# PEER block of 512 tokens on one core: 352 tokens dense and 160 gathered instead of 384 and 128, and V rows stationary in the last matmuls

## The chip, the cores and the metric

One core of a Trainium2 chip runs the whole program; the other cores are idle. The metric is the device time of one execution in microseconds (us), median of several runs.

## The reference, cut to what matters

Two residual blocks run over 512 tokens of width 1024. The change touches only the last part of the second block, a feed-forward layer with 16384 experts (PEER): every token picks 16 experts in each of 8 heads, applies one row of U and one row of V per expert, and sums.

```python
def peer_ffn(h, w_query, sub_keys, u_tab, v_tab):
    q = (h @ w_query).reshape(bsz, seq, 8, 2, 128)
    scores = jnp.einsum('blhcd,hckd->blhck', q, sub_keys)      # 128 keys per half
    s_top, i_top = lax.top_k(scores, 16)
    cand_s = s_top[..., 0, :, None] + s_top[..., 1, None, :]   # 16 x 16 pairs
    cand_i = i_top[..., 0, :, None] * 128 + i_top[..., 1, None, :]
    best_s, pos = lax.top_k(cand_s, 16)
    expert_idx = take_along_axis(cand_i, pos); gates = softmax(best_s)
    # per token: 8 x 16 experts
    act = gelu(einsum('td,thkd->thk', h, u_tab[expert_idx]))
    return einsum('thk,thkd->td', gates * act, v_tab[expert_idx])
x = x + peer_ffn(rms_norm(x), ...)
```

## The kernel before

Everything up to the residual `x3` (features on partitions, 512 tokens along the row) is the same before and after and is not described. What follows computes the PEER layer in two ways at once.

**Dense tokens.** The first TD = 384 tokens are run against all experts. Experts come in NB = 128 blocks of 128. In the U stage each block j is one projection of 8 k-tiles and 3 matmuls each (`mm3`: high weight by high and by low activation, low weight by high activation, so that the products come out in nearly full precision), 24 matmuls with the tokens as moving columns; a gelu writes `act`, which goes to DRAM (`AD`) for 96 blocks and stays in SBUF for the last 32 (`keep`). In the V stage each block n takes its `act`, multiplies it with the gates of the block (`Gg`, zero where a token did not choose the expert), splits the product `w` into `wth` and `wtl`, and multiplies with the 128 rows of V. There `wth` and `wtl` are stationary and the V rows move, 512 columns at a time: for 3 token tiles, 3 products and 2 halves of the width 18 matmuls, into 6 banks of PSUM (`acc`), which are summed over all 128 blocks.

**Gathered tokens.** The last 128 tokens are one token per partition. For each of their 128 choices an indirect DMA on GpSimd's queue (`rows`) fetches one row of U per token, 128 rows of 4 KB; VectorE makes the dot product with `hN` (`gather`), and later scales a row of V and adds it to `accN` (`gather_v`). Ahead of each fetch GpSimd copies one column of a recent `act` into the buffer, which holds the fetch back until that block is done (`pace`); in the V stage this copy is left out. RB = 8 buffers hold fetched rows.

**Routing.** `query` and `scores` compute the 16 query tiles and, on VectorE, the top 16 keys. `choose(t)` picks the experts of token tile t on VectorE, with one product on GpSimd; `dense_gates(t)` builds the gates of a dense tile in DRAM (`GD`), 32 tokens at a time, by four VectorE products (L1428) and 8 small matmuls per 4 tokens (L1411, L1412).

**Weights.** Each 128x1024 weight tile is loaded by a DMA on SyncE's queue (`raw`), rounded by ScalarE (`whi`, L114), and the rest is taken by VectorE (`wlo`, L115). TensorE waits for both.

**Order.** A scheduler orders each engine's queue from the program order and its own cost model. In the program order, every U block also runs RATE_R steps of the routing and RATE_U steps of the gather, every V block RATE_V steps of the gather (`Fill.run`); each step of the gather is one fetch and the use of a fetch made six steps earlier. Until the gathered tokens are routed, a U block runs 3 routing steps.

```python
RATE_R, RATE_U, RATE_V = 1.15, 1.2, 1.08
Gx = Fill(itertools.chain(gather(), gather_v()))
```

Of the kernel before, what the change touches and what calls it, by code (L numbers as in the profile page):

```python
# [26 lines left out]
RB, OB, ABUFS = 8, 2, 3  # L27
# [6 lines left out]
RATE_R, RATE_U, RATE_V = 1.15, 1.2, 1.08  # L34
# [38 lines left out]
def tile_kernel(ctx: ExitStack, tc: tile.TileContext, I, out, dump=None, stop=None):  # L73
# [1159 lines left out]
    TD = 384  # L1233
    NTD = TD // 128
# [6 lines left out]
    hN = gt.tile([128, D], F32, name="hN")  # L1241
    accN = gt.tile([128, D], F32, name="accN")
# [7 lines left out]
    x3d = dr.tile([NTD, 128, D], F32, name="x3d")  # L1250
# [12 lines left out]
    def rows_of_x3(t):  # L1263
        o = accN if t == NTD else n3.tile([128, D], F32, name="x3T", tag="x3T", bufs=2)
# [5 lines left out]
        if t == NTD:  # L1270
            nc.vector.scalar_tensor_tensor(hN, accN, r3[:, t:t + 1], gB, op0=OP.mult, op1=OP.mult)
        else:
            nc.scalar.dma_start(x3d[t], o)

    for t in (NTD, *range(NTD)):
        rows_of_x3(t)
# [50 lines left out]
    def choose(t):  # L1327
# [38 lines left out]
        for i in range(2):  # L1366
            o = rt(f"ii{i}", [8, 16])
            for q in range(2):
                hs = slice(4 * q, 4 * q + 4)
                eq = rt("eq", [4, 16, 16], bufs=2)  # L1370
# [13 lines left out]
        if t == NTD:  # L1384
            nc.vector.tensor_tensor(out=gat.rearrange("p (h k) -> p h k", h=8), in0=g,
                                    in1=gs[:, :, None].to_broadcast([128, 8, 16]), op=OP.mult)
            nc.vector.scalar_tensor_tensor(g.rearrange("p h k -> p (h k)"), res[1], 128.0, res[0],
                                           op0=OP.mult, op1=OP.add)
            nc.vector.tensor_copy(idx, g.rearrange("p h k -> p (h k)"))
            return  # L1390
# [3 lines left out]
        ts = slice(t * 128, (t + 1) * 128)  # L1394
# [4 lines left out]
        nc.scalar.activation(f(R1), pt[:, 0:128], AF.Copy)  # L1399
        nc.scalar.activation(f(R2), pt[:, 128:256], AF.Copy)  # L1400
        nc.scalar.activation(f(GH), pt[:, 256:384], AF.Copy)
        nc.vector.tensor_tensor(out=f(GL), in0=pt[:, 256:384], in1=f(GH), op=OP.subtract)
        yield

    late = []

# [11 lines left out]
    def dense_gates(t, rg):  # L1418
        nb = 128 // GT
        for tb in range(nb * t, nb * t + nb):  # L1420
# [14 lines left out]
        while len(late) > (0 if t == NTD - 1 else 2):  # L1435
            g_mm(*late.pop(0))

    def route():
# [4 lines left out]
        yield from choose(0)  # L1443
        for t in range(NTD):
            nxt = choose(t + 1) if t + 1 < NTD else iter(())
# [7 lines left out]
    def rows(tab, at, paced=True):  # L1453
# [8 lines left out]
    dense_v = []  # L1462

    def gather():
        ready = []
        for k in range(128 + RB - 2):
            if k < 128:
                ready.append((k, rows("peer_u_rows", idx[:, k:k + 1])))
            if k >= RB - 2:
                n, r = ready.pop(0)  # L1470
                nc.vector.scalar_tensor_tensor(r, r, 1.0, hN, op0=OP.mult, op1=OP.mult, accum_out=dot[:, n:n + 1])  # L1471
                if n % 16 == 15:
                    s = slice(n - 15, n + 1)
                    nc.scalar.activation(dot[:, s], dot[:, s], GELU)
                    nc.vector.tensor_tensor(out=dot[:, s], in0=dot[:, s], in1=gat[:, s], op=OP.mult)
            yield

    def gather_v():

        ready = []  # L1480
        for k in range(128 + RB - 2):
            if k < 128:
                ready.append((k, rows("peer_v_rows", idx[:, k:k + 1], not dense_v)))
            if k >= RB - 2:
                n, r = ready.pop(0)
                nc.vector.scalar_tensor_tensor(accN, r, dot[:, n:n + 1], accN, op0=OP.mult, op1=OP.add)  # L1486
            yield

# [43 lines left out]
    for jg in range(NB // AJ):  # L1532
# [11 lines left out]
        for jj in range(AJ):  # L1544
# [10 lines left out]
            if on:  # L1555
                Gx.run(RATE_U)
# [4 lines left out]
    dense_v.append(1)  # L1561
# [140 lines left out]
```

## Time and profile before

| | us |
|---|---|
| median of 3 runs (2893.13 to 2897.28) | 2893.77 |
| the profiled execution, its own time | 2892.62 |
| its span in the trace | 2890.8 |
| outside the span | 1.8 |
| query stage, U stage, V stage, rest (from the trace) | 102.9, 645.8, 559.3, 4.1 |

The stages are those of TensorE: the first matmul of the queries stands at 1578.7 us, the first of U at 1681.6, the first of V at 2327.4, and the last ends at 2886.7. TensorE is busy 96% of the span, VectorE 73%, ScalarE 40%, GpSimd 17%.

### The profile page before, as it was taken

The page shows a single profiled execution, that of the slowest core. Times are in us where ns is not written, and L with a number is a line of the kernel's source. Part 1 is how long each engine was busy: PE and PEld are TensorE (multiplying, and loading weights), DVE is VectorE, ACT ScalarE, POOL GpSimd, SP SyncE. Part 2 cuts the span into 40 slices and gives each one's busy share as a digit, 9 for nine tenths or more (in the row PEclk, how much of TensorE's full clock was granted, in tenths as well). Part 3 has the DMA queues.
Part 4 walks back from the last instruction along what each step waited for, and adds up shares of the span by engine and source line. Part 5 has one row for each costly group of instructions (what it writes and reads, how often), then busy time and mean ns, then how long its engine had stood idle before and what let it go on. Part 6 is the DMA issues. An engine that isn't in the chain of part 4 may idle for free.

```text
span 2890.8 us, 37068 instructions
## 1 busy us (share of the span) xinstructions
PE 2785.8 (96%) x13917; PEld 2280.5 (79%) x13917; DVE 2099.1 (73%) x3645; ACT 1159.4 (40%) x1599; POOL 492.2 (17%) x452
## 2 busy tenths in 40 slices
PE   7999999999999999999999988999998989999999
PEld 5777888877888866656687888898998978777887
DVE  5786894339777665777544999999785579988554
ACT  4667523224333343333433334555553333333332
POOL 0000000000000000000000016546343357652000
PEclk8999999999999999999999999999999999999999
DMA  6333263333333332222233237898899699999663
GB/s 246 122 112 109 97 196 106 124 114 105 97 92 96 89 124 73 73 73 66 75 102 116 88 126 267 299 340 310 323 330 337 234 349 380 401 390 347 216 214 116
DMA packets 167476, 540.11 MB, mean 187 GB/s; under 512 B 16896, under 2 KB 42112, under 8 KB 163840
## 3 DMA queue, kind: packets, MB, share of 16 engines
q1 hardware_dynamic: 128128, 391.94, 39.7%
q0 software_dynamic: 36864, 134.23, 12.5%
q10 hardware_dynamic: 2304, 11.57, 1.1%
q8 instruction: 109, 1.79, 0.2%
q14 instruction: 71, 0.58, 0.1%
HBM read 479.48 MB, written 58.20 MB: 186 GB/s over the span
## 4 chain that ended last, share of the span: by engine, by line
PE 74%; DVE 10%; issue 6%; DMA 5%; POOL 3%; ACT 3%; SPq 0%; DVEq 0%; POOLq 0%; ACTq 0%
PE pmm L122 15%; PE pmm L124 15%; PE pmm L123 15%; PE acc L1604 13%; DMA raw<-in_peer_v_rows_dram 3%; DVE wlo L115 2%; PE pmm L1002 2%; POOL rows L1458 2%; DVE rows L1471 1%; PE pm L209 1%; PE pa L151 1%; POOL rows L1457 1%; PE pg L122 1%; PE pg L123 1%; ACT whi L114 1%
## 5 line engine op out<-in xcount | busy, mean ns | idle before, releaser
L114 ACT ACTIVATE whi<-raw 128x1024 fp32r<-128x1024 f32 (+2 forms) x502 | 518.1, 1033 | 1023.3 <-PE pmm L123 773.4
L115 DVE TENSOR_TENSOR wlo<-raw,whi 128x1024 fp32r<-128x1024 f32 (+2 forms) x502 | 608.0, 1212 | 283.5 <-ACT whi L114 278.9
L124 PE MATMUL pmm<-nph,wlo 128*128 128x384 f32 (+1 forms) x1152 | 398.9, 347 | 20.3 <-DVE wlo L115 20.2
L122 PE MATMUL pmm<-nph,whi 128*128 128x384 f32 (+1 forms) x1152 | 405.7, 352 | 0.3 <-ACT whi L114 0.3
L123 PE MATMUL pmm<-npl,whi 128*128 128x384 f32 (+1 forms) x1152 | 397.5, 345 | 0.0
L1604 PE MATMUL acc<-whi,wth 128*128 128x512 f32 x768 | 243.0, 397 | 7.3 <-ACT whi L114 7.3
L1604 PE MATMUL acc<-wlo,wth 128*128 128x512 f32 x768 | 243.6, 398 | 6.2 <-DVE wlo L115 6.1
L124 PEld LDWEIGHTS pmm<-nph,wlo 128*128 128x128 f32 x1152 | 220.3, 191 | 29.9 <-DVE wlo L115 24.8
L1604 PE MATMUL acc<-whi,wtl 128*128 128x512 f32 x768 | 242.6, 397 | 0.0
L122 PEld LDWEIGHTS pmm<-nph,whi 128*128 128x128 f32 x1152 | 220.6, 192 | 5.1 <-ACT whi L114 0.6
L123 PEld LDWEIGHTS pmm<-npl,whi 128*128 128x128 f32 x1152 | 220.4, 191 | 4.5
L1458 POOL DMA_INDIRECT rows<-in_peer_v_rows_dram,idx x128 | 202.0, 1578 | 108.5 <-DVE accN L1486 97.5
L1471 DVE SCALAR_TENSOR_TENSOR rows<-rows,hN 128x1024 f32<-128x1024 f32 x128 | 155.1, 1218 | 55.3 <-DMA rows<-in_peer_u_rows_dram,idx 55.3
L1486 DVE SCALAR_TENSOR_TENSOR accN<-rows,dot,accN 128x1024 f32<-128x1024 f32 x128 | 163.7, 1279 | 27.3 <-DMA rows<-in_peer_v_rows_dram,idx 27.0
L1604 PEld LDWEIGHTS acc<-wlo,wth 128*128 128x128 f32 x768 | 143.8, 188 | 45.8 <-DVE wlo L115 11.0
L1604 PEld LDWEIGHTS acc<-whi,wth 128*128 128x128 f32 x768 | 144.6, 189 | 44.3 <-ACT whi L114 9.2
L1604 PEld LDWEIGHTS acc<-whi,wtl 128*128 128x128 f32 x768 | 144.8, 189 | 35.8
L1458 POOL DMA_INDIRECT rows<-in_peer_u_rows_dram,idx x128 | 164.0, 1281 | 48.6 <-POOL rows L1457 26.0
L144 ACT ACTIVATE wth<-w 128x384 fp32r<-128x384 f32 x128 | 66.7, 522 | 244.0 <-PE acc L1604 223.7
L145 DVE TENSOR_TENSOR wtl<-w,wth 128x384 fp32r<-128x384 f32 x128 | 70.8, 554 | 101.9 <-ACT wth L144 101.9
L122 PE MATMUL pmm<-h2h,whi 128*128 128x512 f32 x352 | 139.2, 397 | 2.1 <-ACT h2h L186 2.0
L124 PE MATMUL pmm<-h2h,wlo 128*128 128x512 f32 x352 | 138.0, 394 | 2.8 <-DVE wlo L115 2.8
(492 smaller groups left out, 5855.8 us busy)
## 6 DMA issues: line engine op xcount, KB each, us to landing
raw<-in_peer_u_dram SPq DMA_DIRECT2D x128, 512.0 KB, 5.3
raw<-in_peer_v_rows_dram SPq DMA_DIRECT2D x128, 512.0 KB, 6.2
GD<-G SPq DMA_DIRECT2D x12, 2048.0 KB, 11.4
Gg<-GD SPq DMA_DIRECT2D x64, 384.0 KB, 8.5
raw<-in_w_up_dram SPq DMA_DIRECT2D x44, 512.0 KB, 3.5
AD<-act SPq DMA_DIRECT2D x48, 384.0 KB, 6.4
act<-AD SPq DMA_DIRECT2D x48, 384.0 KB, 7.0
raw<-in_w_mod_dram SPq DMA_DIRECT2D x32, 512.0 KB, 3.9
```

Of the source, the lines that this page charges most:

```text
L114: nc.scalar.activation(hi[:, :n], raw[:, :n], AF.Copy)
L115: (eng or nc.vector).tensor_tensor(out=lo[:, :n], in0=raw[:, :n], in1=hi[:, :n].bitcast(F32), op=OP.subtract)
L122: nc.tensor.matmul(ps, wh, ah, start=first, stop=False)
L123: nc.tensor.matmul(ps, wh, al, start=False, stop=False)
L124: nc.tensor.matmul(ps, wl, ah, start=False, stop=last)
L144: nc.scalar.activation(hi, src, AF.Copy)
L145: nc.vector.tensor_tensor(out=lo, in0=src, in1=hi.bitcast(F32), op=OP.subtract)
L1002: nc.tensor.matmul(py[32 * i:32 * i + 32], CD[c][:, s], x, start=n == 0, stop=n == 3)
L1458: nc.gpsimd.indirect_dma_start(out=r, out_offset=None, in_=I[tab], in_offset=bass.IndirectOffsetOnAxis(ap=at, axis=0))
L1471: nc.vector.scalar_tensor_tensor(r, r, 1.0, hN, op0=OP.mult, op1=OP.mult, accum_out=dot[:, n:n + 1])
L1486: nc.vector.scalar_tensor_tensor(accN, r, dot[:, n:n + 1], accN, op0=OP.mult, op1=OP.add)
L1604: nc.tensor.matmul(acc[t][q], a[:, c], bb[:, q * 512:(q + 1) * 512], start=f, stop=l)
```

## The change

352 tokens are dense and 160 gathered. The 32 new gathered tokens (the last 32 rows of tile 2) have 128 choices each; they are put on all 128 partitions as four groups of 32 choices, so that they take 32 fetches of 128 rows more in each of U and V, and their four partial sums are added at the end. The dense matmuls have 352 moving columns in place of 384 in U. In V the rows of V become stationary (8 tiles of 128 features) and `wth`, `wtl` move, 24 matmuls of 352 columns per block into 8 banks, features on partitions; at the end the result is copied out and transposed back. The gates have 11 groups of 32 tokens, not 12. The low halves of the query weights and of the first U block (17 tiles) are made on GpSimd. The fetches in V are held back too, by a mark that ScalarE makes from each `wth`. The routing order becomes tile 3, 2, 0, 1; the rates change; there are 9 row buffers; `eq` is fp16; `hN` and `accN` share a buffer.

```diff
-RB, OB, ABUFS = 8, 2, 3
+RB, OB, ABUFS = 9, 2, 3
-RATE_R, RATE_U, RATE_V = 1.15, 1.2, 1.08
+RATE_R, RATE_U, RATE_U2, RATE_V = 1.25, 1.1, 1.7, 1.45
-    TD = 384
-    NTD = TD // 128
+    TD = 352
+    NTD = 3
+    TX = 128 * NTD - TD
...
     def rows_of_x3(t):
...
+        elif t == NTD - 1:
+            p = slice(128 - TX, 128)
+            nc.vector.scalar_tensor_tensor(hX[p], o[p], r3[p, t:t + 1], gB[p], op0=OP.mult, op1=OP.mult)
+            for c in range(3):
+                nc.scalar.dma_start(hX[TX * c:TX * c + TX], hX[p])
+        nc.scalar.dma_start(x3d[t], o)
...
-            get_w(*(("w_query", x) if x < 16 else ("peer_u", x - 16)))
+            get_w(*(("w_query", x) if x < 16 else ("peer_u", x - 16)), eng=nc.gpsimd)
...
+            for c in range(4):
+                for d, x in ((idxX, ix), (gatX, ga)):
+                    nc.gpsimd.dma_start(d[TX * c:TX * c + TX], x[128 - TX:128, 32 * c:32 * c + 32])
...
-        for tb in range(nb * t, nb * t + nb):
+        for tb in range(nb * t, min(nb * t + nb, NTB)):
...
-        if paced:
-            nc.gpsimd.tensor_copy(r[:, 0:1], pace[0])
+        nc.gpsimd.tensor_copy(r[:, 0:1], pace[0])
...
+    places = [(idx, gat, dot, k) for k in range(128)] + [(idxX, gatX, dotX, k) for k in range(32)]
...
     def gather_v():
+        accN = gt.tile([128, D], F32, name="accN", tag="hN")
+        nc.gpsimd.dma_start(accN, x3d[NTD])
+        accX = gt.tile([128, D], F32, name="accX", tag="hX")
+        nc.gpsimd.memset(accX, 0.0)
+        nc.gpsimd.dma_start(accX[0:TX], x3d[NTD - 1, 128 - TX:128])
...
+        for c in range(1, 4):
+            r = gt.tile([128, D], F32, name="rows", tag="rows", bufs=RB)
+            nc.gpsimd.dma_start(r[0:TX], accX[TX * c:TX * c + TX])
+            nc.vector.tensor_tensor(out=accX[0:TX], in0=accX[0:TX], in1=r[0:TX], op=OP.add)
+        nc.gpsimd.dma_start(out[TD:128 * NTD], accX[0:TX])
...
-                Gx.run(RATE_U)
+                Gx.run(RATE_U2 if R.done else RATE_U)
...
-    acc = [[ps.tile([128, 512], F32, name=f"acc{t}{q}", bufs=1) for q in range(2)] for t in range(NTD)]
+    acc = [ps.tile([128, 512], F32, name=f"acc{k}", tag=f"acc{k}", bufs=1) for k in range(KT)]
...
+        m = vp.tile([128, 1], F32, name="mark", tag="mark", bufs=16)
+        nc.scalar.activation(m, wth[:, 0:1].bitcast(F32), AF.Copy)
+        marks.append(m)
...
-        for t in range(NTD):
-            c = slice(t * 128, (t + 1) * 128)
-            for a, bb, f, l in ((wth, vh, n == 0, False), (wth, vl, False, False), (wtl, vh, False, n == NB - 1)):
-                for q in range(2):
-                    nc.tensor.matmul(acc[t][q], a[:, c], bb[:, q * 512:(q + 1) * 512], start=f, stop=l)
+        pace[0] = marks[max(n - 2, 0)]
+        last.append((n, w, wth, wtl, vh, vl))
+        if n != NB - 2:
+            for k in range(KT):
+                s = slice(k * 128, (k + 1) * 128)
+                for m, _, wth, wtl, vh, vl in last:
+                    pq = acc[k][:, :TD]
+                    nc.tensor.matmul(pq, vh[:, s], wth, start=m == 0, stop=False)
+                    nc.tensor.matmul(pq, vh[:, s], wtl, start=False, stop=False)
+                    nc.tensor.matmul(pq, vl[:, s], wth, start=False, stop=m == NB - 1)
+                if n == NB - 1:
...
+                    if k % 2:
+                        nc.vector.tensor_copy(yT[:, k], acc[k][:, :TD])
+                    else:
+                        nc.scalar.activation(yT[:, k], acc[k][:, :TD], AF.Copy)
+            last.clear()
         Gx.run(RATE_V)
     Gx.run(1000)
-    nc.sync.dma_start(out[TD:T], accN)
...
+            for k in range(4):
+                nc.tensor.transpose(pt[:m, k * 128:(k + 1) * 128], yT[:, 4 * q + k, t * 128:t * 128 + m], ident)
...
+            nc.vector.tensor_tensor(out=x3[:m, t, c], in0=pt[:m], in1=x3[:m, t, c], op=OP.add)
+            nc.sync.dma_start(out[t * 128:t * 128 + m, c], x3[:m, t, c])
```

## Rows read from the trace of the kernel before

**Rows 1.** The page: the span, and each engine's busy time, share and instructions

```profile
span 2890.8 us, 37068 instructions
...
PE 2785.8 (96%) x13917; PEld 2280.5 (79%) x13917; DVE 2099.1 (73%) x3645; ACT 1159.4 (40%) x1599; POOL 492.2 (17%) x452
```

**Rows 2.** Windows: length, busy us of PE, PEld, DVE, ACT, POOL; clock, DMA, GB/s

```profile
1578.70:1681.60 102.90, 102.12 (x514) 86.36 (x513) 95.99 (x478) 37.20 (x56) 0.00 (x0) 1.00 0.28 93
1681.60:2002.00 320.40, 291.15 (x1864) 279.49 (x1863) 317.37 (x739) 151.57 (x192) 163.81 (x146) 0.96 0.78 277
2002.00:2192.00 190.00, 178.22 (x1221) 170.20 (x1220) 155.37 (x233) 97.92 (x125) 82.37 (x89) 0.97 0.91 330
2192.00:2327.40 135.40, 134.43 (x773) 134.11 (x772) 73.26 (x84) 47.21 (x67) 47.00 (x61) 0.99 0.76 267
2327.40:2380.00 52.60, 43.65 (x175) 33.23 (x174) 38.32 (x47) 14.75 (x21) 32.51 (x23) 0.97 1.00 378
2380.00:2644.00 264.00, 259.46 (x1092) 205.63 (x1091) 248.05 (x285) 93.72 (x123) 160.47 (x95) 0.99 1.02 390
2450.00:2550.00 100.00, 99.62 (x426) 79.40 (x425) 94.59 (x109) 34.14 (x45) 67.84 (x40) 1.00 1.03 398
2644.00:2886.70 242.70, 242.67 (x1041) 194.14 (x1039) 129.70 (x173) 84.10 (x111) 0.00 (x0) 1.00 0.59 193
```

**Rows 3.** Timeline of TensorE's matmuls in the U stage: start, duration, instruction

```profile
1990.32 0.33 PE L124 MATMUL pmm<-nph,wlo 128*128 128x384 f32 x1
...
1992.39 0.34 PE L124 MATMUL pmm<-nph,wlo 128*128 128x384 f32 x1
...
1993.02 0.42 PE L122 MATMUL pmm<-nph,whi 128*128 128x384 f32 x1
1993.28 0.34 PE L123 MATMUL pmm<-npl,whi 128*128 128x384 f32 x1
```

**Rows 4.** Timeline of TensorE's matmuls in the V stage

```profile
2700.31 0.63 PE L1604 MATMUL acc<-whi,wth 128*128 128x512 f32 x2
...
2704.98 0.39 PE L1604 MATMUL acc<-wlo,wth 128*128 128x512 f32 x1
```

**Rows 5.** Timeline of TensorE's matmuls of 256 columns, in the attention part

```profile
1114.83 0.28 PE L1064 MATMUL pmm<-wlo,hbh 128*128 128x256 f32 x1
...
1115.78 0.28 PE L1063 MATMUL pmm<-whi,hbh 128*128 128x256 f32 x1
```

**Rows 6.** Timeline of the weight loads of those matmuls

```profile
1114.83 0.19 PEld L1065 LDWEIGHTS pmm<-whi,hbl 128*128 128x128 f32 x1
```

**Rows 7.** TensorE's waits in the U stage: us in total, times, longest

```profile
PE pmm L124 <- DVE wlo L115: 20.2, 10, 6.6
```

**Rows 8.** Windows of VectorE's gate products (L1428) alone, 1681.6 to 2192

```profile
1681.60:2192.00 510.40, 132.68 (x192) 0.97 0.83 296
```

**Rows 9.** Timeline of VectorE in the V stage

```profile
2441.60 1.22 DVE L115 TENSOR_TENSOR wlo<-raw,whi 128x1024 fp32r<-128x1024 f32 x1
2442.74 0.55 DVE L1583 TENSOR_TENSOR w<-keep,Gg 128x384 f32<-128x384 f32 x1
2443.20 1.28 DVE L1486 SCALAR_TENSOR_TENSOR accN<-rows,dot,accN 128x1024 f32<-128x1024 f32 x1
2444.40 0.55 DVE L145 TENSOR_TENSOR wtl<-w,wth 128x384 fp32r<-128x384 f32 x1
```

**Rows 10.** Groups of GpSimd in the whole span: busy us, mean ns

```profile
L1373 POOL TENSOR_TENSOR eq<-eq,idf 128x1024 f32<-128x1024 f32 x12 | 36.2, 3021 | 26.1 <-DVE eq L1371 26.1
```

**Rows 11.** Groups of GpSimd in the V stage

```profile
L1458 POOL DMA_INDIRECT rows<-in_peer_v_rows_dram,idx x115 | 189.3, 1646 | 104.0 <-DVE accN L1486 97.5 <-issue 6.0 <-DVE wtl L145 0.3
```

**Rows 12.** Timeline of transposes ahead of the queries, and of the last instructions

```profile
1573.94 5.02 PE L1268 MATMUL pmm<-ident,x 128*128 128x128 f32 x32
...
2883.68 4.09 DVE L1611 TENSOR_TENSOR x3b<-acc,x3b 128x512 f32<-128x512 f32 x6 [7.25 <-PE acc L1604]
```

**Rows 13.** The page's DMA issues: KB each, us to landing

```profile
Gg<-GD SPq DMA_DIRECT2D x64, 384.0 KB, 8.5
```

More of the change, by code (lines that the diff above doesn't have):

```diff
@@ L1263, in rows_of_x3 @@
     def rows_of_x3(t):
-        o = accN if t == NTD else n3.tile([128, D], F32, name="x3T", tag="x3T", bufs=2)
+        o = n3.tile([128, D], F32, name="x3T", tag="x3T", bufs=2)
         for q in range(2):
@@ L1270, in rows_of_x3 @@
         if t == NTD:
[L1271 to L1275, printed above, removed]
+            nc.vector.scalar_tensor_tensor(hN, o, r3[:, t:t + 1], gB, op0=OP.mult, op1=OP.mult)
+        elif t == NTD - 1:
[4 more added lines that the diff above has]
+        nc.scalar.dma_start(x3d[t], o)
+    for t in range(NTD, -1, -1):
         rows_of_x3(t)
@@ L1434, in dense_gates @@
                     yield
-        while len(late) > (0 if t == NTD - 1 else 2):
+        while len(late) > (0 if t == seq[-1] else 2):
             g_mm(*late.pop(0))
@@ L1442, in route @@
         rg = rx_.enter_context(tc.tile_pool(name="rg", bufs=1, side="right", reuse_waits="tile"))
-        yield from choose(0)
-        for t in range(NTD):
-            nxt = choose(t + 1) if t + 1 < NTD else iter(())
+        yield from choose(seq[0])
+        for n, t in enumerate(seq):
+            nxt = choose(seq[n + 1]) if n + 1 < NTD else iter(())
             for i, _ in enumerate(dense_gates(t, rg)):
@@ L1460, in rows @@
         return r
[L1462 removed]
+    places = [(idx, gat, dot, k) for k in range(128)] + [(idxX, gatX, dotX, k) for k in range(32)]
     def gather():
         ready = []
[L1466 to L1468 removed]
+        for k in range(len(places) + RB - 2):
+            if k < len(places):
+                ix, ga, do, n = places[k]
+                ready.append((ga, do, n, rows("peer_u_rows", ix[:, n:n + 1])))
@@ L1476, in gather @@
             yield
     def gather_v():
+        accN = gt.tile([128, D], F32, name="accN", tag="hN")
[3 more added lines that the diff above has]
+        nc.gpsimd.dma_start(accX[0:TX], x3d[NTD - 1, 128 - TX:128])
         ready = []
-        for k in range(128 + RB - 2):
-            if k < 128:
-                ready.append((k, rows("peer_v_rows", idx[:, k:k + 1], not dense_v)))
+        for k in range(len(places) + RB - 2):
+            if k < len(places):
+                ix, ga, do, n = places[k]
+                ready.append((do, n, rows("peer_v_rows", ix[:, n:n + 1])))
@@ L1484, in gather_v @@
             if k >= RB - 2:
-                n, r = ready.pop(0)
-                nc.vector.scalar_tensor_tensor(accN, r, dot[:, n:n + 1], accN, op0=OP.mult, op1=OP.add)
-            yield
+                do, n, r = ready.pop(0)
+                a = accN if do is dot else accX
+                nc.vector.scalar_tensor_tensor(a, r, do[:, n:n + 1], a, op0=OP.mult, op1=OP.add)
+            if k == 128 + RB - 2:
+                nc.gpsimd.dma_start(out[128 * NTD:T], accN)
+            yield
+        for c in range(1, 4):
+            r = gt.tile([128, D], F32, name="rows", tag="rows", bufs=RB)
+            nc.gpsimd.dma_start(r[0:TX], accX[TX * c:TX * c + TX])
+            nc.vector.tensor_tensor(out=accX[0:TX], in0=accX[0:TX], in1=r[0:TX], op=OP.add)
```

62 lines of the change are left out of this document (36 added, 26 removed).

## The prediction

> **What bounds the kernel now.** I read the page first: TensorE's matmuls are busy 96% of the span, VectorE 73%, ScalarE 40% [rows 1], so the question is what TensorE does and why it idles. Then the windows by stage [rows 2]. The reader is to see three regimes there. In the U stage up to 2002 us VectorE is busy 317.4 of 320.4 us, so it sets the pace; from 2002 to 2192 both are high; from 2192, where the gates are done, TensorE alone is full (134.4 of 135.4). In the V stage until 2644, as long as gathered rows come in, DMA is at a share of 1.00 to 1.03 and VectorE at 94% of 2380 to 2644; after that TensorE is full and all else has room. The waits say the same: TensorE's longest wait in U is for VectorE's low halves of the weights, 20.2 us, up to 6.6 us at a time [rows 7].
>
> Then the timelines, for the period from one matmul's start to the next, since the listed durations overlap. 384 columns: 12 periods between 1990.32 and 1992.39, 0.1725 us each [rows 3]. 512 columns in V: 20 periods in 4.67 us, 0.2335 us [rows 4]. 256 columns: 8 periods in 0.95 us, 0.119 us [rows 5].
>
> **The matmuls.** From 256 to 384 columns the period grows by 0.00042 us a column, so 352 columns should take 0.159 us, 24 of them 3.82 us. A U block takes 24 x 0.1725 = 4.14 now. A V block takes 18 x 0.2335 = 4.20. By the slope 512 columns would take 0.226; in V they take 0.007 more, where every matmul goes to another bank than the last. After the change the bank changes at every third, at most 8 x 0.007 = 0.06 a block: 3.82 to 3.88, I take 3.85. So TensorE's own work falls by 128 x 0.32 = 41 us in U and 128 x 0.35 = 45 us in V. The gate matmuls of 4 tokens cost 0.545 us (0.89 from 1992.39 to 1993.28 less two periods) [rows 3]; 88 in place of 96 save 4 us.
>
> One rule speaks against this. In the last part of U the weight loads are busy 134.1 of 135.4 us, and V goes from 18 to 24 loads a block [rows 2]. The Trainium skill ("Perfetto Trace Analysis", Identifying the Most-Contended Engine) takes the busy share of weight loads as the measure of TensorE's headroom, and by it U has none. A load is listed with 0.19 us but follows the last after 0.119 us where the matmuls have 256 columns [rows 5, 6], so loads overlap one another, and I don't take them as a bound; the case is rival 3.
>
> **The U stage, by VectorE.** In program order the routing has 109 steps after the gathered tokens are routed at block 3, done at 1.15 a block by block 95 or so. With 11 token groups it has 102, and at 1.25 is done by block 84. Up to 2192 VectorE was busy 317.4 + 155.4 = 472.8 of 510.4 us, 92.6% [rows 2]. Off this go: 12 low halves (84 blocks, not 96) at 1.14 from start to start, 14 us [rows 9]; some 21 dot products (1.1 x 81 = 89 against 110) at 1.20, the price of the like operation in V, 25 us [rows 9]; a twelfth of the gate products' 132.7 us, 11 us [rows 8]; and the lag with which VectorE enters the stage. In the query stage it was 96.0 of 102.9 us busy [rows 2], 16 low halves (18 us) of which go to GpSimd; I take 8 us of lag saved, bounds 0 and 18. Left are 415 us. TensorE needs 84 x 3.82 + 88 x 0.545 = 369 in this part, so VectorE still sets it: 415 if it never idles, 448 at the 92.6% of before; I take 432. The new rates ask for more VectorE work per block than before, which is why the gain of the matmuls is not all kept here.
>
> The other 44 blocks: the 32.2 blocks (773/24) after 2192 took 4.20 each against 4.14 of matmuls, 1.5% more [rows 2]. So 44 x 3.82 x 1.015 = 171 us. At 1.7 fetches a block VectorE needs 1.14 + 1.7 x 1.20 = 3.2 of 3.82 us, and DMA 0.524 x 2.7 = 1.42 MB, 370 GB/s, under the 398 that the trace shows [rows 2]. U: 432 + 171 = 603 us in place of 645.8, bounds 583 (415 + 168) and 628 (448 + 180).
>
> **The V stage.** 5 steps of the U gather and 167 of the V gather are left, at 1.45 a block 119 of the 128 blocks. Per block in that time: TensorE 3.85; VectorE 1.14 for the low half, 2 x 0.46 x 352/384 for `w` and `wtl`, 1.45 x 1.20 for the adds, 3.74 us [rows 9]; DMA 0.524 MB of V rows, 0.760 of gathered rows, 0.180 of gates (a block's share of four 384 KB loads, less a twelfth) and 0.135 of `act`, 1.60 MB [rows 13], which at 398 GB/s is 4.02 us. That 398 was moved while TensorE was 99.6% and VectorE 94.6% busy [rows 2], with GpSimd waiting for VectorE to free row buffers (97.5 us in all) [rows 11], so it is not shown to be the ceiling. VectorE at 94.6% gives 3.95, between 3.85 and 4.02; I take that. 119 x 3.95 + 9 x 3.85 = 505, and 5 for the start, where TensorE idled 9 of 52.6 us while fetches ran unheld [rows 2]. 510 us against 559.3. Bounds: 495 with TensorE never waiting, and 119 x 4.50 + 35 = 570 at the pace of before, which made 70.4 blocks (1267/18) in the 316.6 us with gathers [rows 2].
>
> The whole stage moves 119 x 1.60 + 9 x 0.5, some 195 MB. The Trainium skill ("HBM Reference", Specifications) gives a core some 358 GB/s, by which V would take an estimated 545 us and the sum would be 2837; the 398 of rows 2 is above that, and the page itself lets a core that streams alone go higher.
>
> **What costs nothing, and under what cover.** GpSimd's 17 low halves: 3.02 us each by its nearest product [rows 10], 51 us in a stage of 102.9 in which it did nothing [rows 2]; a tile is prepared two query tiles ahead, over 10 us, and if that cover is gone each costs up to 1.9 us more than on VectorE. I take 1 us gained before U, bounds 3 either way. `hX` and its three DMAs on ScalarE's queue wait for VectorE; behind them stand the next copies, with ScalarE 36% busy [rows 2]: 0, at most 3. The eight small DMAs of choices stand on GpSimd's queue and wait for `choose`; behind them wait fetches, and behind those dot products. GpSimd is half busy there [rows 2], and the buffers hold 7 fetches, some 30 us: 0, at most 10. `accN` and `accX` are loaded on GpSimd's queue between the last U dot and the first V fetch: the 7 steps without a fetch cover it. The marks are one ScalarE column a block: 0. SyncE loses one output DMA to GpSimd.
>
> **The end.** Now 4.1 us pass after the last matmul. After: a copy of 0.55, 12 transposes at 5.02/32 = 0.16, an add of 0.68 [rows 12], 3 us of landing as now, latencies: 6.5.
>
> **Sum**, against the profiled execution's 2892.6 (1.1 under the median): 1680.6 to U, 603, 510, 6.5, and 1.8 outside the span: 2802 us.
>
> **Rivals.** 1. TensorE sets both stages: VectorE at 100% in U (583), 495 in V, in all 2767. For it: from 2450 to 2550 TensorE was 99.6% busy at a DMA share of 1.03 [rows 2]. Against: VectorE at 97%, DMA and TensorE must then all fit within 3.85 us. 2. The gather takes the gain of V: a fetch late by DMA stops VectorE in its queue, then low halves, then TensorE, and V keeps 4.50 a block: 570, in all 2862. For it: DMA at 1.03 already and 25% more rows; against: fetches are now held back, so no bursts. 3, the other side: weight loads bind. At 0.188 us each a block costs 4.51 in both stages: U 432 + 44 x 4.51 = 630, V 128 x 4.51 + 5 = 582, in all 2901, slower. It decides in V from 0.175 us a load (4.20/24); rows 5 show 0.119. 4. The gather outlasts the matmuls: the 115 fetches in V took 2.75 us each before (in 316.6 us) [rows 11], by which 165 take 454 us; 12 us of sums at the end leave 498, so it shows from 3.0 us a fetch and makes the kernel slower from 3.6.
>
> **How the numbers follow.** Forecast 0.60 (its own range 2785 to 2825), rival 1 0.15, rival 2 0.15, rival 3 0.05, rival 4 0.05 (half of it slower). Range: from rival 1 to short of rival 2's end, 2766 to 2858, leaving rivals 3 and 4 and half of 2 outside. 0.2%, 6 us, is about what can be told from no change. Faster 0.91, same 0.02, slower 0.07.
>
> **What would show it.** Right: 352-column periods near 0.159 us in both stages; gates done by block 84 or so; the first V matmul near 2284 us; VectorE near full in the first part of U; V near 510 us with the last gathered add some 35 us before the end; no waits for low halves in the first blocks of U beyond some 10 us. Wrong: periods near 0.188; TensorE waiting in V for `wlo` behind adds that wait for DMA; an end that waits for `accX`.

## The result and the profile after

The changed kernel takes 2931.68 us (median of 4 runs, 2924.05 to 2940.7); the kernel before took 2893.45 beside it (4 runs). The ratio is 1.0126, 95% interval 1.0105 to 1.0147: slower, where 2802 us was forecast. The profiled execution took 2934.4 us. Against the terms of the sum:

| | forecast | measured | difference |
|---|---|---|---|
| start of U | 1680.6 | 1699.6 | +19.0 |
| U | 603 | 628.3 | +25.3 |
| V, to its last matmul | 510 | 596.1 | +86.1 |
| end, after that | 6.5 | 8.6 | +2.1 |
| outside the span | 1.8 | 1.8 | 0 |

First the page, then the windows by stage (length, then busy us of PE, PEld, DVE, ACT, POOL; clock, DMA share, GB/s), to be held against [rows 1, 2].

```profile
span 2932.6 us, 39249 instructions
...
PE 2749.0 (94%) x14645; PEld 2339.0 (80%) x14645; DVE 2127.6 (73%) x3721; ACT 1164.1 (40%) x1725; POOL 731.6 (25%) x726
```

```profile
1584.60:1699.60 115.00, 104.90 (x515) 88.30 (x513) 81.36 (x467) 37.79 (x57) 33.62 (x15) 0.96 0.30 96
1699.60:2020.00 320.40, 279.16 (x1883) 266.34 (x1882) 307.77 (x744) 152.88 (x198) 148.83 (x142) 0.94 0.75 266
2166.00:2326.90 160.90, 148.61 (x888) 145.56 (x886) 116.04 (x165) 50.73 (x76) 112.60 (x125) 0.97 0.95 351
2327.90:2926.60 598.70, 536.16 (x3096) 522.40 (x3096) 462.58 (x559) 211.61 (x389) 358.13 (x327) 0.94 0.88 318
2380.00:2740.00 360.00, 321.13 (x1829) 313.47 (x1827) 286.40 (x339) 126.10 (x229) 245.62 (x220) 0.92 0.94 338
```

The last two rows hold most of the story. From 2380 to 2740 us gathered rows come in, and yet nothing is full: TensorE 89% busy, VectorE 80%, DMA 0.94, where before it stood at 1.02 as long as rows came in [rows 2]. TensorE made 1829/24 = 76.2 blocks in these 360 us, 4.72 us a block, and its matmuls alone would have needed 3.85. So it waits, and the waits in the V stage say for what (us in total, times, longest):

```profile
DVE accN L1511 <- DMA rows<-in_peer_v_rows_dram,idx: 73.3, 22, 8.4
...
DVE accX L1511 <- DMA rows<-in_peer_v_rows_dram,idxX: 18.6, 6, 9.4
DVE accN L1511 <- POOL rows L1473: 8.2, 3, 6.4
...
PE acc L1644 <- DVE wtl L145: 48.9, 23, 7.5
PE acc L1645 <- DVE wlo L115: 12.6, 20, 0.7
...
POOL rows L1473 <- ACT mark L1622: 118.7, 40, 10.1
```

VectorE waits some 100 us for gathered rows, 92 us of them in 28 waits of 3.3 us on average (in the kernel before it was 7.7 us in 2 waits, the line below); TensorE's 61 us are for the two things that VectorE makes behind those adds; and GpSimd's fetches wait 118.7 us for ScalarE's marks, which the kernel before did not have.

```profile
DVE accN L1486 <- DMA rows<-in_peer_v_rows_dram,idx: 7.7, 2, 6.6
```

The groups of VectorE from 2380 to 2740 (busy us, mean ns, idle before) show that this is its only idleness: 286.40 + 73.6 = 360.0.

```profile
L1511 DVE SCALAR_TENSOR_TENSOR accN<-rows,dot,accN 128x1024 f32<-128x1024 f32 x111 | 141.9, 1279 | 73.6 <-DMA rows<-in_peer_v_rows_dram,idx 65.3 <-POOL rows L1473 8.2
L115 DVE TENSOR_TENSOR wlo<-raw,whi 128x1024 fp32r<-128x1024 f32 x76 | 92.4, 1216 | 0.0
L145 DVE TENSOR_TENSOR wtl<-w,wth 128x352 fp32r<-128x352 f32 x76 | 39.2, 516 | 0.0
```

One such wait in the timelines (start, duration, instruction, idle before it). The parts are GpSimd, VectorE and TensorE:

```profile
2450.38 6.00 POOL L1473 COPY rows<-mark 128x1 f32<-128x1 f32 x2 [1.25 <-ACT mark L1622]
2456.52 3.85 POOL L1474 DMA_INDIRECT rows<-in_peer_v_rows_dram,idx  x1
2460.68 0.94 POOL L1474 DMA_INDIRECT rows<-in_peer_v_rows_dram,idx  x1 [0.31 <-issue]
2461.62 0.20 POOL L1473 COPY rows<-mark 128x1 f32<-128x1 f32 x1
...
2459.02 0.51 DVE L145 TENSOR_TENSOR wtl<-w,wth 128x352 fp32r<-128x352 f32 x1
2467.96 1.28 DVE L1511 SCALAR_TENSOR_TENSOR accN<-rows,dot,accN 128x1024 f32<-128x1024 f32 x1 [8.43 <-DMA rows<-in_peer_v_rows_dram,idx]
...
2471.41 0.66 PE L1644 MATMUL acc<-wtl,whi 128*128 128x352 f32 x1 [6.54 <-DVE wtl L145]
...
2473.01 0.49 PE L1643 MATMUL acc<-wth,whi 128*128 128x352 f32 x1
2473.30 0.50 PE L1644 MATMUL acc<-wtl,whi 128*128 128x352 f32 x1
...
2477.49 0.32 PE L1644 MATMUL acc<-wtl,whi 128*128 128x352 f32 x1
2477.65 0.33 PE L1645 MATMUL acc<-wth,wlo 128*128 128x352 f32 x1
```

An add stands at the head of VectorE's queue from 2459.5 on; its row has not come. The next `w`, `wtl` and `wlo` stand behind it; once the add is done they start without a further wait. TensorE then lacks `wtl` for 6.54 us, and when it goes on, its matmuls follow each other at 0.29 us until 2477 and at 0.16 after that: it comes back at the lower of its two clock levels, 1.2 GHz (granted clock 0.50 from 2467.1 to 2477.1 us, 1.00 after that). So a wait is paid about one and a half times. V has some 75 us at the lower level (10 before). In 16 of them TensorE stands still anyway; in the other 59 it works at half speed, which costs some 29 us. The matmuls themselves (128 x 3.85 = 493), TensorE's waits for VectorE (61) and this (29) make 583 of the 596 us.

In the traces GpSimd was done with issuing the median V fetch 16.2 us ahead of its add before, with 7 fetches ahead of the adds; now it is 8.0 us, with 3. The queue's order is fixed beforehand from the scheduler's modelled times.

The query stage is longer too, 115.0 against 102.9 us [rows 2], though VectorE does less in it (81.4 us against 96.0). TensorE's wait there, and ScalarE's queue:

```profile
PE pmm L1328 <- DMA sk<-in_sub_keys_dram: 9.5, 1, 9.5
```

```profile
1589.55 1.16 ACTq L1281 DMA_DIRECT2D hX<-hX  x2
...
1594.90 0.33 ACTq L1282 DMA_DIRECT2D x3d<-x3T  x1
...
1598.38 0.34 ACTq L1297 DMA_DIRECT2D sk<-in_sub_keys_dram  x1
```

The sub-keys `sk` lie where `x3T` lay and can be loaded only when the last store of `x3T` is through. The copies of `hX` stand ahead of that store on the same queue. The load is issued at 1598.4, where before it went out at 1567.8, and TensorE, after 9.5 us without it, ran at a mean clock of 0.69 from 1604 to 1614.

### The profile page after: what moved, and what is told of

Its sections match the earlier page's. It is cut to its first block, busy times and chain, and to the rows that moved or that the text cites. A ratio compares the mean times of both kernels' runs of the same rounds, so it can differ in the third digit from the quotient of the medians.

```text
span 2932.6 us, 39249 instructions
## 1 busy us (share of the span) xinstructions
PE 2749.0 (94%) x14645; PEld 2339.0 (80%) x14645; DVE 2127.6 (73%) x3721; ACT 1164.1 (40%) x1725; POOL 731.6 (25%) x726
## 4 chain that ended last, share of the span: by engine, by line
PE 55%; issue 16%; POOL 14%; DVE 9%; DMA 3%; ACT 2%; POOLq 0%; DVEq 0%; SPq 0%; ACTq 0%
PE pmm L122 13%; PE pmm L124 13%; PE pmm L123 13%; POOL rows L1474 10%; POOL rows L1473 4%; PE pmm L1002 2%; DVE wlo L115 2%; PE pm L209 1%; PE acc L1645 1%; PE acc L1643 1%; PE pa L151 1%; PE acc L1644 1%; DVE rows L1488 1%; PE pg L122 1%; PE pg L123 1%
## 5 line engine op out<-in xcount | busy, mean ns | idle before, releaser
L124 PE MATMUL pmm<-nph,wlo 128*128 128x352 f32 (+1 forms) x1152 | 391.2, 340 | 41.7 <-DVE wlo L115 41.7
L122 PE MATMUL pmm<-nph,whi 128*128 128x352 f32 (+1 forms) x1152 | 396.4, 345 | 1.1 <-ACT whi L114 1.1
L1644 PE MATMUL acc<-wtl,whi 128*128 128x352 f32 x1024 | 344.1, 336 | 48.9 <-DVE wtl L145 48.9
L123 PE MATMUL pmm<-npl,whi 128*128 128x352 f32 (+1 forms) x1152 | 389.2, 338 | 0.0
L1645 PE MATMUL acc<-wth,wlo 128*128 128x352 f32 x1024 | 344.8, 337 | 12.8 <-DVE wlo L115 12.6
L1643 PE MATMUL acc<-wth,whi 128*128 128x352 f32 x1024 | 343.0, 335 | 1.9 <-ACT wth L144 1.0
L1644 PEld LDWEIGHTS acc<-wtl,whi 128*128 128x128 f32 x1024 | 201.9, 197 | 56.0 <-DVE wtl L145 56.0
L1645 PEld LDWEIGHTS acc<-wth,wlo 128*128 128x128 f32 x1024 | 201.6, 197 | 18.9 <-DVE wlo L115 18.9
L1643 PEld LDWEIGHTS acc<-wth,whi 128*128 128x128 f32 x1024 | 201.8, 197 | 2.5 <-ACT wth L144 1.3
L1473 POOL COPY rows<-mark 128x1 f32<-128x1 f32 x160 | 129.4, 826 | 119.2 <-ACT mark L1622 118.7
```

What stands on the lines that cost most here:

```text
L122: nc.tensor.matmul(ps, wh, ah, start=first, stop=False)
L123: nc.tensor.matmul(ps, wh, al, start=False, stop=False)
L124: nc.tensor.matmul(ps, wl, ah, start=False, stop=last)
L1643: nc.tensor.matmul(pq, vh[:, s], wth, start=m == 0, stop=False)
L1644: nc.tensor.matmul(pq, vh[:, s], wtl, start=False, stop=False)
L1645: nc.tensor.matmul(pq, vl[:, s], wth, start=False, stop=m == NB - 1)
```

## The experiments

Times are medians; "before" was run beside each group, at 2893.57, 2895.91, 2896.08 and 2896.39 us. V and U are lengths from the profiles, each from its first matmul to its last. Between the two stages another 4.3 us pass in e10, 3.9 in e5 and 2.0 in e14, elsewhere at most 0.6. e7, e13 and e14 leave out part of the result.

| run | us | ratio to before, 95% | U | V |
|---|---|---|---|---|
| e1 V fetches free | 2879.57 | 0.9945 (0.9925 to 0.9966) | 634.4 | 540.2 |
| e2 copies that wait for nothing | 2892.81 | 0.9994 (0.9980 to 1.0009) | 630.8 | 555.5 |
| e11 old kernel, held | 2882.57 | 0.9953 (0.9937 to 0.9969) | 641.5 | 546.4 |
| e15 hold looser, old U rates | 2898.15 | 1.0013 (0.9996 to 1.0029) | 618.2 | 570.9 |
| e13 held, half adds | 2888.08 | 0.9964 (0.9950 to 0.9978) | 630.3 | 551.5 |
| e14 free, half adds | 2936.41 | 1.0129 (1.0106 to 1.0151) | 632.5 | 597.0 |
| e7 free, half the V tiles | 2845.78 | 0.9821 (0.9794 to 0.9847) | 633.5 | 507.9 |
| e3 old kernel, V rows stationary | 2901.51 | 1.0023 (1.0010 to 1.0037) | 641.3 | 562.6 |
| e4 query lows on VectorE | 2925.66 | 1.0098 (1.0078 to 1.0118) | 632.6 | 585.6 |
| e5 e1, `hX` on SyncE's queue | 2878.39 | 0.9932 (0.9914 to 0.9950) | 634.4 | 540.1 |
| e10 e1, sub-keys early | 2875.67 | 0.9931 (0.9916 to 0.9947) | 639.4 | 542.2 |
| e6 e1, U fetches held less | 2871.86 | 0.9913 (0.9896 to 0.9931) | 623.1 | 539.5 |
| e8 e1, old U rates | 2867.74 | 0.9895 (0.9876 to 0.9913) | 617.0 | 541.7 |
| e9 e6 and e8, lows on VectorE | 2872.69 | 0.9910 (0.9888 to 0.9933) | 610.8 | 550.9 |
| e12 e9, 1.35 steps in V | 2872.60 | 0.9919 (0.9902 to 0.9936) | 610.9 | 553.6 |
| e16 e8 and e10 | 2861.00 | 0.9882 (0.9861 to 0.9902) | 620.3 | 545.4 |

The first theory was: the hold (each V fetch waits for a mark of ScalarE) makes rows late, and VectorE, in its fixed order, passes that on. The rivals were that the new form of the matmuls costs time, that the gather's DMA takes V's gain (rival 2), and that the copies on GpSimd are the price.

**e1.** The changed kernel; V fetches are not held.

```diff
-        nc.gpsimd.tensor_copy(r[:, 0:1], pace[0])
+        if paced:
+            nc.gpsimd.tensor_copy(r[:, 0:1], pace[0])
...
-                ready.append((do, n, rows("peer_v_rows", ix[:, n:n + 1])))
+                ready.append((do, n, rows("peer_v_rows", ix[:, n:n + 1], not dense_v)))
```

> The changed kernel with one part undone: in the V stage the row fetches are not held back by marks (no copy ahead of a fetch), as before. Theory (the hold takes away the lead of the fetches, so VectorE, which works strictly in order, waits for rows that land late, 103 us of waits in V, and TensorE then waits for wtl and wlo): the waits of the adds for landings fall from 103 us to some 30, V falls from 599 us to 515 (505 to 535), the time from 2932 to about 2848. Rival (DMA is full, and 25% more rows simply take that long): V stays at 580 to 600 and the time at 2920 or more. Rival (VectorE and GpSimd obstruct one another through the copies): as the theory here, told apart by the next run.

**e2.** The copies stay, from a constant.

```diff
-        pace[0] = marks[max(n - 2, 0)]
+        pace[0] = epsb
```

> The changed kernel with the copies ahead of the V fetches kept, but reading a constant instead of a mark, so that GpSimd has the same instructions and none of them holds a fetch back. Theory (the hold takes the lead away): V falls to 515 to 540 us as without the copies, the time to 2850 to 2870. Rival (the copies themselves, and the locks they share with VectorE, cost the time): V stays at 575 to 600. Rival (DMA is full): V stays at 580 to 600 here and in the run before alike.

**e3.** The kernel before with the rows of V stationary, still 384 columns: the loops of the changed kernel in place of L1604's, and its transposes at the end.

> The kernel before with one part of the change alone: V rows stationary, 24 matmuls of 384 columns a block, and the transposes at the end; 384 tokens dense, rates, fetches and lows as before. Theory (the form itself is sound, and its period is that of the columns): a block 24 x 0.1725 = 4.14 us in place of 4.20, 8 us less in V, 2.5 us more at the end, so 2888 (2880 to 2895). Rival (24 weight loads of 0.188 us set the block): 4.51 us a block, 40 us more, 2933.

The hold costs 56 us of V (596.1 to 540.2), of which the wait in the copy is some 40 (596.1 to 555.5) and the copies themselves 15. The medians differ by 52 us; the changed kernel's V code took 585.6 in e4's profile, so up to 10 us of the 56 may be spread from build to build. With free fetches the median fetch is issued 21.4 us ahead, and VectorE is idle 2.2 us in all ahead of V adds. In e3 an undisturbed block takes 4.16 us against 4.20, nowhere near 4.51, so rival 3 falls. Its forecast of 2880 to 2895 missed all the same: 2901.51, 0.2% over before. The end takes 7.5 us against 4.1, and V as a whole 3 more than before, since TensorE waits 18 us in it for VectorE and ScalarE (13 before). And e1's V of 540 is neither the 510 of the prediction nor in e1's own 505 to 535, as e2's 555.5 is over its 515 to 540.

**e11.** The counter-test that followed: the old kernel with the hold alone.

```diff
-                ready.append((k, rows("peer_v_rows", idx[:, k:k + 1], not dense_v)))
+                ready.append((k, rows("peer_v_rows", idx[:, k:k + 1])))
...
+        m = vp.tile([128, 1], F32, name="mark", tag="mark", bufs=16)
+        nc.scalar.activation(m, wth[:, 0:1].bitcast(F32), AF.Copy)
+        marks.append(m)
...
+        pace[0] = marks[max(n - 2, 0)]
```

> The kernel before, with one thing of the change alone: its V fetches are held back by ScalarE's marks. Theory (a held fetch lands after its add stands at the head of VectorE's queue, whatever the form of the matmuls): VectorE waits some 60 us or more ahead of V adds where it waited 27, V goes from 559 us to 580 or more, total 2912 to 2935 us. Rival (the hold hurts only because the changed kernel has a quarter more fetches and a fuller VectorE): V within 8 us of 559, total 2890 to 2902 us.

Both expectations missed: the same hold makes the old kernel faster, V 546.4 in place of 559.3. Its window from 2380 to 2740 and its VectorE group:

```profile
2380.00:2740.00 360.00, 360.00 (x1544) 289.91 (x1544) 301.56 (x354) 138.31 (x257) 173.89 (x186) 1.00 0.96 346
```

```profile
L1486 DVE SCALAR_TENSOR_TENSOR accN<-rows,dot,accN 128x1024 f32<-128x1024 f32 x93 | 119.2, 1282 | 55.7 <-DMA rows<-in_peer_v_rows_dram,idx 53.9 <-POOL rows L1457 1.4
```

VectorE waits for rows here too: 70 us ahead of the adds in V by the trace, 19 more ahead of those that come before V starts. But per block (1544/18 = 85.8 of them) it has 3.51 us of work and 0.68 of idle time, 4.20 together, and the matmuls take 4.20: TensorE is busy 360.00 of 360. What it gains is that the weights are no longer late: from 2331 to 2645 ScalarE waited 99.2 us for V tiles before, and waits 4.1 us now.

```profile
ACT whi L114 <- DMA raw<-in_peer_v_rows_dram: 99.2, 35, 10.0
```

```profile
ACT whi L114 <- DMA raw<-in_peer_v_rows_dram: 4.1, 2, 2.6
```

In the changed kernel it is 286.4/76.2 = 3.76 of work and 0.97 of idle time, 4.72, over matmuls of 3.85. The first theory was only half of it: late rows cost nothing while VectorE has room for the wait.

**e7, e14: what keeps V at 540 with free fetches.** In e7 a V tile is loaded only for every second block and used twice; in e14 an add works on 512 columns.

```diff
-        return w, wth, wtl, *load_w(I["peer_v_rows"][j * 128:(j + 1) * 128])
+        if n % 2 == 0:
+            half[0] = load_raw(I["peer_v_rows"][j * 128:(j + 1) * 128], 1024)
+        return w, wth, wtl, *split_w(half[0], 1024)
```

```diff
-                nc.vector.scalar_tensor_tensor(a, r, do[:, n:n + 1], a, op0=OP.mult, op1=OP.add)
+                h = slice(0, 512)
+                nc.vector.scalar_tensor_tensor(a[:, h], r[:, h], do[:, n:n + 1], a[:, h], op0=OP.mult, op1=OP.add)
```

> The run with V fetches free, which loads a tile of V rows only for every second block and uses it twice, so that the result is not that of all rows: this leaves out 64 DMAs of 512 KB, a sixth of the bytes of V, and no instruction of the engines. Theory (with the fetches free what is left of the loss in V is DMA, 387 to 398 GB/s): V falls from 540 to 505 to 515 us, the time to 2845 to 2855. Rival (VectorE's strict order and its 90% load set V): V stays at 530 or more, the time at 2870 or more.

> The same halved adds with V fetches that nothing holds back. Theory (with the fetches free, V's loss against 510 is DMA at its ceiling and not VectorE, which is busy 333 of 360 us): V stays within 10 us of 540, total 2870 to 2882 us. Rival (VectorE at 92.5% is the bound): V 515 us or less, total near 2853.

The windows of e1, at the start of V and over the same 360 us; of e7 over these; and of e14 during the gather and after it:

```profile
2326.60:2380.00 53.40, 44.31 (x237) 42.34 (x237) 41.33 (x55) 17.91 (x36) 28.60 (x23) 0.88 1.02 386
...
2380.00:2740.00 360.00, 347.34 (x2093) 340.97 (x2092) 333.08 (x389) 140.44 (x257) 198.53 (x133) 0.98 1.02 392
```

```profile
2380.00:2740.00 360.00, 359.30 (x2225) 358.82 (x2225) 356.11 (x419) 151.92 (x277) 204.98 (x136) 1.00 0.96 354
```

```profile
2380.00:2670.00 290.00, 242.05 (x1329) 232.91 (x1330) 206.88 (x302) 91.83 (x168) 163.53 (x134) 0.89 1.03 400
...
2740.00:2860.00 120.00, 120.00 (x748) 120.00 (x747) 68.00 (x94) 51.34 (x95) 0.00 (x0) 1.00 0.69 230
```

With half of the V tiles, a sixth of the DMA of a block, gone, TensorE is full at 360/92.7 = 3.88 us a block, with VectorE 99% busy and the gather as fast as in e1: V is 507.9 us, inside the 505 to 515 expected. So it is DMA. e14 says it the other way round, and neither expectation saw it coming: less work on VectorE makes V 57 us longer. Faster adds free the row buffers sooner, a fetch goes out every 290/134 = 2.16 us in place of 360/133 = 2.71, DMA is at 400 GB/s, and the loads of the dense V tiles lose. ScalarE's wait for them, in e14 until 2670, in e1 until 2785 and in the changed kernel until 2840:

```profile
ACT whi L114 <- DMA raw<-in_peer_v_rows_dram: 175.4, 35, 13.9
```

```profile
ACT whi L114 <- DMA raw<-in_peer_v_rows_dram: 172.0, 49, 12.5
```

```profile
ACT whi L114 <- DMA raw<-in_peer_v_rows_dram: 34.1, 8, 8.4
```

In e1 most of that wait was covered: VectorE waited 24.5 us in V for ScalarE's rounded tiles, in e14 170.4 us.

```profile
DVE wlo L115 <- ACT whi L114: 24.5, 14, 2.2
```

```profile
DVE wlo L115 <- ACT whi L114: 170.4, 69, 8.5
```

As soon as the gather of e14 ends, TensorE is full.

**e13, e15, e12: between hold and no hold.** e13 is the changed kernel with e14's edit of the add; e15 has the rates of before in U and

```diff
-        pace[0] = marks[max(n - 2, 0)]
+        pace[0] = marks[max(n - 5, 0)]
```

e12 has free fetches and `RATE_V` 1.35 in place of 1.45.

> The changed kernel, V fetches held as in it, but each V add works on 512 of its 1024 columns (the other half of the gathered result is left out). Theory (the hold makes fetched rows late in every kernel; it costs TensorE time only where VectorE's work and its waits together exceed the matmuls, in the changed kernel 286.4 us of work and 73.6 of waits in the 76 blocks of 2380 to 2740 us, 4.74 us a block against 3.85): with some 0.9 us of work a block less, V falls from 596 to 510 to 535 us although the fetches stay held, total 2845 to 2870 us. Rival (the held fetch itself sets the pace, through GpSimd's queue or the row buffers, whatever VectorE has to do): V stays at 575 or more, total 2910 or more.

> The changed kernel with the rates of before in U and V fetches held by the mark of five blocks back, not of two. Theory (three blocks more lead, some 11 us, let the rows land before their add, and DMA is still spread out): VectorE waits under 50 us ahead of V adds, V at 541 us or below, total 2850 to 2866. Rival (the adds are placed in VectorE's queue where the planner's model has them landed, so a longer lead only moves them forward): waits near 100 us, V at 580 or more, total 2905 or more.

> The combined version with one number changed: 1.35 steps of the gather per V block in place of 1.45. Theory (with the fetches free, what V still loses is DMA: 1.60 MB a block at 398 GB/s are 4.02 us, over TensorE's 3.85; at 1.35 it is 1.55 MB and 3.89 us): V near 520 us where the combined version has 540, total some 15 us under that. Rival (the fetches run ahead of their steps anyway, as far as buffers allow, so the step rate does not set the DMA rate, or the last adds come behind the last matmul): within 5 us of the combined version, or slower than it by the adds at the end.

e13 got 45 of the 60 to 85 us expected. VectorE is idle longer ahead of V adds (132.5 us), and DMA is at 1.01:

```profile
2380.00:2740.00 360.00, 338.94 (x2043) 333.44 (x2042) 258.19 (x376) 140.01 (x255) 206.66 (x245) 0.98 1.01 378
```

So room on VectorE is most of what the hold lacks; that DMA comes next is argued from its share alone. e15 fell between its two sides: 72.6 us of idle time ahead of adds, V 571, worse than no hold (541.7 in e8). In e12 the fetches ran as before (the last at 2781 against 2777), as the rival had it: with nothing to hold them, row buffers set the rate, not steps. A version that spreads the gather evenly without stopping VectorE was not found.

**e4, e5, e10: the query stage.** e4 is the changed kernel without `eng=nc.gpsimd`. e5 is e1 with the copies of `hX` on SyncE's queue. e10 is e1 with

```diff
-RB, OB, ABUFS = 9, 2, 3
+RB, OB, ABUFS = 7, 2, 3
...
+    sk = gt.tile([128, 16, 128], F32, name="sk")
+    nc.scalar.dma_start(sk, I["sub_keys"])
...
-    sk = rt("sk", [16, 128], pool=rq)
-    nc.scalar.dma_start(sk, I["sub_keys"])
```

> The changed kernel with the 17 low halves of query weights back on VectorE. Theory (moving them helped U by freeing VectorE early, and the 12 us lost in the query stage come from the late load of the sub keys, which waits for the buffer that x3T held): the query stage still has its wait of some 9.5 us for that load, VectorE enters U some 15 us behind, and the time grows by 5 to 20 us to 2937 to 2952. Rival (GpSimd's slower low halves, 2.4 us each, cost the query stage its time): the query stage falls by 10 us or more and the time to 2922 or less.

> The run with V fetches free, and the three DMAs that copy hX moved from ScalarE's queue to SyncE's. Theory (ScalarE's queue stands behind these DMAs, which wait for VectorE and for one another; x3T is copied and stored late, and the sub keys, whose buffer lies where x3T lay, come 9.5 us late to the first scores): TensorE's wait for the sub keys falls from 9.5 us to 0 to 3, the query stage from 115 to 103 to 106 us, the time from 2880 to 2868 (2865 to 2873). Rival (the late load has its cause in the larger buffers alone, whatever the queue): no change, 2880.

> The changed kernel with V fetches that nothing holds back, and with the sub-keys in a buffer of their own, loaded early, so that their load no longer waits for the gathered tokens' norm to leave the buffer; the room for it is taken from two of the nine row buffers. Theory (the query stage is 12 us longer because TensorE waits 9.5 us for the sub-keys and its clock falls to half after that): query stage about 103 us, no wait for sub-keys, U starts some 11 us earlier, total near 2869 us, up to 6 more for the two buffers. Rival (the longer query stage comes from the low halves on GpSimd or the extra gathered tokens' work on VectorE): the stage stays at 111 us or more, total 2880 or above.

Low halves on GpSimd gain nothing: without them the query stage is 115.1 us and V starts at 2327.8, as with them (2327.9), and the time is 6 us lower if anything (intervals overlap), between the two expectations. e5 takes the wait for the sub-keys from 9.5 to 5.9 us and the stage to 111.6, far from the 103 to 106 expected; its total is e1's. e10 takes all of it: 103.0 us, TensorE 102.37 busy at clock 1.00.

```profile
1577.10:1680.10 103.00, 102.37 (x515) 86.32 (x513) 81.48 (x466) 37.76 (x57) 33.48 (x14) 1.00 0.31 97
```

So the longer stage was the buffer, and only some 3.5 us of it the copies on ScalarE's queue. Of the 12 us little was left in e10's total, 4 us in the medians (the intervals overlap) and not the 11 expected: in the profiles U grew by 5, the pause between U and V by 4 and V by 2.

**e6, e8, e9, e16: the U stage.** e6 is e1 with `PB = 3` (a U fetch waits for a block three earlier); e8 is e1 with the rates of before (1.15, 1.2, 1.2); e9 has both and e4's edit; e16 is e8 with e10's edit.

> The run with V fetches free, and in U each fetch held by the block three before the present one, not by the present one. Theory (in U as in V the hold takes the lead from the fetches): VectorE's waits for rows in U fall from 71 us to 40 or less, the U stage from 634 to 610 to 622 us, the time to 2858 to 2870. Rival (U is set by the amount of VectorE work in its first part): U stays within 5 us of 634 and the time within 6 of 2880.

> The run with V fetches free, and the rates of U as before the change: routing 1.15 a block, fetches 1.2 a block throughout. Theory (VectorE's work sets the first part of U, and 1.25 and 1.1 against 1.15 and 1.2 hardly change its sum per block): U within 8 us of 634, and the 160 fetches of U end some 15 blocks into V, so that V grows by 10 to 30 us: 2890 (2880 to 2910). Rival (the faster routing crowds VectorE early and costs U its gain): U falls by 15 us or more, to 618 or less.

> The changed kernel with V fetches that nothing holds back, U fetches held until one block earlier less (three blocks in all), the rates of before in U (1.15, 1.2, 1.2) and the low halves of the query weights on VectorE again. Theory (the U stage loses by two separate things, the fetch rate after the gates and the lateness of held fetches): some 617 us of U less another 5, V 540, about 2858 us, 35 us under the kernel before. Rival (both edits relieve the same wait of VectorE for fetched rows, so that only the larger counts): U 617, about 2867 us, as with the rates alone.

> The changed kernel with free V fetches, the rates of before in U and the sub-keys loaded early into a buffer of their own (seven row buffers). Theory (the query stage and the rates are separate losses): some 10 us under the version with those rates alone, 2856 to 2862 us. Rival (VectorE sets U, and the time that the query stage saves comes back as waits for rows in U with two buffers less, as 5 of the 11 us did with the faster rates): 2863 to 2870 us.

The faster rates cost 17 us of U, against a forecast of at most 8; a looser hold gives 11, about as expected. Together U came to 610.8, as the theory had it, but V took 9 to 11 us more than in e8 and e6, and the total went nowhere (2872.69, where 2858 was forecast; runs from 2859.28 to 2876.07). What in V took it back wasn't settled. e16 is the fastest that computes everything, 35 us under before and 71 under the change as it was made.

## Why the prediction was wrong

**The step that failed is "The marks are one ScalarE column a block: 0".** It priced the instruction and not what it does. A hold moves every V fetch, and the adds that use them stand in a queue whose order doesn't move along. Measured, that is 56 us of V (e1), 65% of the miss there; VectorE's idle time ahead of adds in the V stage went from 7.9 to 102.9 us. My upper bound of V, the old pace of 4.50 a block, was no bound for that reason: the new pace was 4.72.

**The V term beside that.** I took 3.95 a block between 3.85 (TensorE) and 4.02 (1.60 MB at 398 GB/s) because 398 was "not shown to be the ceiling". e14 shows DMA at 400 GB/s with the V tiles starved, and e1 took 360/87.2 = 4.13 at 392: the upper bound was the value to take. 97 blocks at 4.13, 21 at 3.85 after the gather and the first 53.4 us with their 10 blocks make 535 of the 540. VectorE's 3.74 a block (the terms add up to 3.72) was 3.82 in e1 (333.1/87.2), so at 3.85 it had no room for any wait at all. I noted 94.6% for it and did not ask what a wait of VectorE would then cost.

**Rival 2 had the chain, not the cause, and too low a price (570 against 596).** "A fetch late by DMA stops VectorE in its queue, then low halves, then TensorE" is what the waits show, but what made the fetch late was the hold, which I had counted against that rival ("fetches are now held back, so no bursts"). That sentence is right by itself: in e11 the hold takes DMA from 1.02 to 0.95 between 2380 and 2644 and V gains 13 us. It is false that it comes free.

The prediction set the 358 GB/s of the Trainium skill ("HBM Reference", Specifications) against the trace. No run here is bound at that figure; the page's other statement, that a core streaming alone goes well above the share, agrees with the 400 GB/s of e14. The estimate that the prediction worked out from that figure, 545 us for V, lies near what free fetches gave (540.2), but by luck: e1 moved 387 GB/s from 2340 to 2785 and 162 after that, 358 in neither.

**The query stage: "0, at most 3" and "1 us gained".** 12.1 of the 19 us of late start are in this stage (and 1 is the gain that I had counted), and e10 shows their cause: a load that waited for the buffer of `x3T`. The copies of `hX` ahead of it are some 3.5 us of that (e5). I had looked at what stands behind the copies on ScalarE's queue, not at whose buffer waits for that. The GpSimd low halves gained nothing (e4). The other 6 us arose ahead of the changed code; the experiments with the same code there started the queries at 1577.1 to 1585.4, so it is put down to no part of the change.

**U: 432 and 171.** The gates were done at block 85 after 437.5 us (block 84 and 432 forecast). The other 43 blocks took 190.8 us, not 171: I added 1.5% to the matmuls as before, but in this part VectorE waited 53.7 us for held rows and TensorE 16.0 us for the low halves behind them, the same chain as in V. With the rates of before, U is 617 (e8), with the looser hold as well 611 (e9), inside my bounds of 583 to 628; 603 was never reached. The 3.2 of 3.82 us that VectorE was to need there left out waits again.

**What was right.** Matmuls of 352 columns follow at 0.160 us in U and 0.161 in V, and undisturbed blocks take 3.84 to 3.87 us in both (0.159, 3.82 and 3.85 forecast). Weight loads don't bind: in e7 they are busy 358.82 of 360 us while TensorE keeps 3.88 us a block, far from 4.51. The Trainium skill ("Perfetto Trace Analysis", Identifying the Most-Contended Engine) names their busy share as one measure of TensorE's headroom. In these traces it tells little of it: TensorE was as full at a share of 0.80 (194.14 of 242.70 us, the end of V before) as at 0.99 (the end of U before) [rows 2], and at 0.99 there was still room for the step from 0.1725 to 0.160 us a load. The end, 8.6 us, is near.

**What stays open.** The runs show that the hold lengthens V only where VectorE is full, and that without it the V tiles are late. How much of the held rows' lateness is the mark and how much GpSimd's slow copies and fetches beside VectorE is split only by e2 (40 and 15), and e2 brought the bursts back with it.

## What to carry to other kernels

Before costing a throttle on prefetches, ask how far ahead the data now lies and what stands behind its user in an in-order queue: a hold is free only while that engine's work and its new waits together stay under the period of the engine that sets the pace. When a stage has three resources within 8% of each other (here 3.74, 3.85 and 4.02 us a block), making one faster (shorter matmuls, shorter adds) can make the whole slower, through the resource that two streams share. A small new DMA is costed by every buffer whose release waits for it, not by its queue alone.

## What the hardware showed beyond that

GpSimd's instructions stretch beside VectorE's two-input ones. In the timeline above a copy of one column takes 0.20 us and a fetch 0.94 while VectorE stands still, and 3 us (6.00 for two) and 3.85 while it runs adds and differences back to back. These are the extremes: over the V stage, copies beside a VectorE that was busy throughout took 0.86 us in the median (99 of them), beside an idle one 0.19 (57); fetches took 1.30 (71) and 0.95 (50). So a late row makes the next fetches quick, and a busy VectorE makes them slower. The Trainium skill ("SBUF — State Buffer", Who interferes with whom) has a VectorE instruction with two inputs in SBUF contend with a GpSimd instruction that reads there, and calls the contention an exclusive lock. The trace agrees that the two kinds collide, but the longest fetch is 2.9 us longer, more than any one VectorE instruction beside it takes (at most 1.28 us); what else held it isn't shown.

At 400 GB/s the two streams of V do not slow down alike: in e14 the gather still made a fetch every 2.16 us, while ScalarE waited up to 13.9 us for one dense tile.
